# Linear attention: a pair's state updates one piece ahead of its outputs, and row tiles loaded one half per piece

## The chip, the core and the metric

The kernel runs on one NeuronCore of a Trainium2 chip. TensorE (PE in the profile; PEld is its weight load) multiplies matrices into PSUM; VectorE (DVE), ScalarE (ACT) and GpSimd (POOL) work on tiles element by element; SyncE (SP) issues most of the DMA transfers, ScalarE's queue some of them. Each engine takes its own instructions in order, and semaphores hold an instruction until its operands are there and its output buffer is free. The metric is the device time of one execution in microseconds (us), the median of several.

## The reference, cut to what matters

One decoder layer: a normalised input goes through one large projection, then through two branches side by side (a state space model, SSD, and a gated linear attention, GLA), which are gated, merged, projected and added to the input. The change lies in the linear attention and in how the normalised input is made. Per head, with the sequence cut into chunks:

```python
def step(s, inp):
    qi, ki, vi, gi = inp                       # gi: cumulated log gates of the chunk
    o_inter = einsum('bhtk,bhkv->bhtv', qi * exp(gi), s)
    att = ...                                  # causal, decayed q k products in the chunk
    o_intra = einsum('bhts,bhsv->bhtv', att, vi)
    g_last = gi[:, :, -1]
    k_dec = ki * exp(g_last[:, :, None, :] - gi)
    s_new = exp(g_last)[..., None] * s + einsum('bhsk,bhsv->bhkv', k_dec, vi)
    return s_new, o_inter + o_intra
```

So a chunk's output needs the state `s` from before the chunk, and the state goes on by a decay and an increment that depends on keys and values alone. The input of the branches is `u = x * rsqrt(mean(x*x) + eps) * w`, row by row. Sequence 2048 plus 16 meta tokens, model width 1024, 4 GLA heads with 128 key and 256 value channels, 16 SSD heads in 4 groups.

## The kernel before, in words

The sequence is cut into four blocks of 512 rows (the first has the 16 meta rows as well), and a block into four chunks of 128. The program has two halves.

The **first half** goes over the blocks. For each block it goes over eight units: four SSD groups (`ssd_proj`) and four GLA heads (`gla_proj`). A unit is mostly projections: TensorE multiplies weight tiles (`whl`, loaded by SyncE in `load_w`) with the normalised block `u`, in three matmuls per product (`accum`, L185 to L187: high by high, high by low, low by high). A unit is written as a generator that yields six times, that is, in six *pieces*. After every piece the loop calls `step()`, which advances each generator in `running` by one of its own pieces: the scan of the unit before (`ssd_scan` or `gla_scan`), the load of the next block (`fetch_u`, which runs `load_u`, begun with the first GLA head), and sums for the second half. A scan of a head h is begun when its projections are over, so its piece 1 stands behind the first projection piece of head h+1, its piece 7 behind the first projection piece of head h+2, beside piece 1 of the next scan. The last scan of all is begun earlier, within its own head.

TensorE and SyncE keep exactly this written order (`manual_schedule`). The order of ScalarE, VectorE and GpSimd is set by a planner that simulates the program with its own costs.

`gla_scan` of one head: pieces 1 to 5 build the attention matrix in six levels (`level_in`: L688 to L695 on VectorE, L691 and L692 on ScalarE; `level_out`: two matmuls L703 into a `pc` bank, merged by L710), and turn the decayed keys around (`turn_keys`, L724, giving `kdt`). Piece 6 transposes the odd chunks of the attention matrix (L790) and splits them into `atp`. Pieces 7 and 8 take a pair of chunks each:

- six matmuls `kdt` by values into a `pc` bank, the increments of the two chunks;
- for the first chunk the state update L805 on VectorE (old state times decay plus increment) into a tile `c1` (the profile calls it `c`), the output's matmul with the old state (L808), three matmuls with the first chunk's attention, three with the second's;
- last the matmul with the new state (L811). The second update writes `s_gla`, the state's own tile.

Then ScalarE copies the outputs (L812) and squares them (L815). PSUM has two `pc` banks; they are used by `level_out`, by the increments, by the outputs and by the SSD scan (L564 and L567).

`load_u` of a block behind the first: in each of four pieces it loads one row chunk in two halves of 512 columns (L258, tile `acc`, two buffers, which the convolution of the SSD groups uses too), squares each half with a row sum on ScalarE (L259), adds the sums (L260) and raises the mean to the power -1/2 (on GpSimd). Then one piece turns the row factors into a broadcast tile (L280), and eight pieces load one feature tile each (L294), scale it (L296), write its high part (L298) and its low part (L300) and store it (L299).

`dt_chain`, once per block, computes step sizes and their cumulated sums with four small scratch tiles of the pool `sm` and writes the block's tiles `tkd`, `tkc`, `wde`, `ecu`, `dec`.

The **second half** (from L876) is a series of large products from operands in DRAM. Its tiles take the memory of the first half's. Between the halves the last two scans end beside a few first products (`between`).

Of the kernel before, what the change touches and what calls it, by code (L numbers as in the profile page):

```python
# [7 lines left out]
F32 = mybir.dt.float32  # L8
# [3 lines left out]
AF = mybir.ActivationFunctionType  # L12
ALU = mybir.AluOpType

P = 128
D = 1024
KT = 8
META = 16
BLK = 512
NCH = BLK // P  # L20
# [5 lines left out]
NSQ = 5  # L26
NT4 = 5
NACT = 8
NC1 = 6
LEVELS = (64, 32, 16, 8, 4, 2)  # L30
NMSK = len(LEVELS) + 1
QSCALE = 128.0 ** -0.5
# [8 lines left out]
def trunk_kernel(ctx: ExitStack, tc: tile.TileContext, xm, xmt, w_feat, w_tok, w_zm, w_br, w_o,  # L41
                 cf32, cmsk, pvec, fnw, hvec, gw2, out):
    nc = tc.nc
# [5 lines left out]
    def mk(pool, shape, dt, tag, **kw):  # L49
        cnt[0] += 1  # L50
        return pool.tile(shape, dt, tag=tag, name=f"{tag}_{cnt[0]}", **kw)
# [52 lines left out]
    for s in range(nsb):  # L104
        b = 2 * s + 2
# [16 lines left out]
    bpool, wk, sm, const = pool1("bpool", 1), pool1("wk", 2), pool1("sm", 4), pool1("const", 1)  # L122
    pj = ctx.enter_context(tc.tile_pool(name="pj", bufs=3, space=bass.MemoryType.PSUM))
    pt = ctx.enter_context(tc.tile_pool(name="pt", bufs=3, space=bass.MemoryType.PSUM))
    pc = ctx.enter_context(tc.tile_pool(name="pc", bufs=2, space=bass.MemoryType.PSUM))

    def bank(pool, tag):
        return mk(pool, [P, 512], F32, tag)
# [20 lines left out]
    s_gla = const.tile([P, GH, 256], F32, name="s_gla")  # L149
# [33 lines left out]
    def accum(ps, stat, mov, first, last, **kw):  # L183
        (sh, sl), (mh, ml) = stat, mov
        nc.tensor.matmul(ps, sh, mh, start=first, stop=False, **kw)  # L185
        nc.tensor.matmul(ps, sh, ml, start=False, stop=False, **kw)  # L186
        nc.tensor.matmul(ps, sl, mh, start=False, stop=last, **kw)  # L187
# [44 lines left out]
    def split(h, lo, src):  # L232
        nc.scalar.activation(h, src, AF.Copy)
        nc.vector.tensor_tensor(lo, src, h.bitcast(F32), op=ALU.subtract)


    def load_u(b):
        m0 = META if b == 0 else 0
        row0 = META - m0 + b * BLK
        tt = m0 + BLK  # L240
        pair = mk(upool, [P, 2, KT * (META + BLK)], F32R, "u")[:, :, :KT * tt]
        uh, ul = [pair[:, i].rearrange("p (k t) -> p k t", k=KT) for i in range(2)]

        def rows_rstd(r0, n, vector=False):
            ss = mk(sm, [P, 1], F32, "ss")
            if m0:
                xt = mk(wk, [P, D], F32, "tok4", bufs=NT4)
                nc.sync.dma_start(xt[:n], xm[r0:r0 + n, :])
                if vector:
                    nc.vector.scalar_tensor_tensor(xt[:n], xt[:n], 1.0, xt[:n], op0=ALU.mult, op1=ALU.mult,  # L250
                                                   accum_out=ss[:n])
                else:
                    nc.scalar.activation(xt[:n], xt[:n], AF.Square, accum_out=ss[:n])
            else:
                s2 = mk(sm, [P, 2], F32, "ss2")
                for i in range(2):
                    xt = mk(wk, [P, META + BLK], F32, "acc")[:, :BLK]
                    nc.sync.dma_start(xt, xm[r0:r0 + n, i * BLK:(i + 1) * BLK])  # L258
                    nc.scalar.activation(xt, xt, AF.Square, accum_out=s2[:, i:i + 1])  # L259
                nc.vector.tensor_tensor(ss, s2[:, 0:1], s2[:, 1:2], op=ALU.add)  # L260
            r = mk(sm, [P, 1], F32, "rs1")
            nc.vector.tensor_scalar(r[:n], ss[:n], 1.0 / D, EPS, op0=ALU.mult, op1=ALU.add)
            nc.gpsimd.tensor_tensor(r[:n], r[:n], mhalf[:n, 0:1], op=ALU.pow)
            return r

        rs = []
        if m0:
            rm_s = rows_rstd(0, META, True)
        for c in range(NCH):
            rs.append(rows_rstd(META + b * BLK + c * P, P, c % 2))  # L270
            yield
        if m0:
            rs.append(rm_s)
            nc.sync.dma_start(cst[:, :2], cf32[:, :2])
            nc.sync.dma_start(pv, pvec)
            for q in range(NWR):
                raws[f"zm_{q}"] = load_raw(w_zm[:, q * 288:(q + 1) * 288])
        rb = bank(pt, "pt")
        for c in range(NCH):
            nc.tensor.matmul(rb[:, c * P:(c + 1) * P], rs[c].to_broadcast([P, P]), ident, start=True, stop=True)  # L280
        rbs = [(rb, m0, BLK)]
        if m0:
            rm = bank(pt, "pt")
            nc.tensor.matmul(rm[:, :META], rs[NCH][:META].to_broadcast([META, P]), ident[:META, :META],
                             start=True, stop=True)
            rbs = [(rm, 0, META)] + rbs
        else:
            rbc = mk(wk, [P, 3 + META + BLK], F32, "cin")[:, :BLK]
            nc.scalar.activation(rbc, rb, AF.Copy)
            rbs = [(rbc, 0, BLK)]  # L290
            yield
        for kt in range(KT):
            xk = mk(wk, [P, META + BLK], F32, "act" if m0 else "acc", bufs=NACT if m0 else 2)[:, :tt]
            nc.sync.dma_start(xk, xmt[:, kt, row0:row0 + tt])  # L294
            for ps, a, n in rbs:
                nc.vector.scalar_tensor_tensor(xk[:, a:a + n], xk[:, a:a + n], norm_w[:, kt:kt + 1], ps[:, :n],  # L296
                                               op0=ALU.mult, op1=ALU.mult)
            nc.scalar.activation(uh[:, kt, :tt], xk, AF.Copy)  # L298
            nc.scalar.dma_start(u_left[b][kt], xk[:, m0:])  # L299
            nc.vector.tensor_tensor(ul[:, kt, :tt], xk, uh[:, kt, :tt].bitcast(F32), op=ALU.subtract)  # L300
            yield
        return uh, ul
# [62 lines left out]
    def dt_chain(o, psd):  # L365
        m0, nck, ci0 = o.m0, o.nck, o.ci0
        tkd, tkc, wde, ecu, dec = o.tkd, o.tkc, o.wde, o.ecu, o.dec

        def t80(tag):
            return mk(sm, [P, 5, NH], F32, tag, bufs=1)[:, :nck]  # L370

        x = t80("dx")
        for i in range(nck):
            nc.vector.tensor_tensor(x[:, i], psd[i][:, 256:272], hv[:, 0], op=ALU.add)
            nc.scalar.activation(
                o.alr[:, i].rearrange("p (r c) -> p r c", c=16),
                psd[i][:, 272:288].unsqueeze(1).to_broadcast([P, 3, 16]), AF.Copy)
        e = t80("de")
        nc.scalar.activation(e, x, AF.Abs)
        nc.scalar.activation(e, e, AF.Exp, scale=-1.0)  # L380
        w1 = t80("dw")
        nc.vector.tensor_scalar(w1, e, 1.0, None, op0=ALU.add)
        ln = t80("dl")
        nc.scalar.activation(ln, w1, AF.Ln)
        nc.vector.scalar_tensor_tensor(e, w1, 1.0, e, op0=ALU.subtract, op1=ALU.subtract)
        nc.vector.tensor_tensor(ln, ln, e, op=ALU.subtract)
# [8 lines left out]
        if m0:  # L395
            nc.tensor.matmul(ps[:, :NH], ones[:META], x[:META, 0], start=True, stop=True)
        nc.tensor.matmul(ps[:, ci0 * NH:nck * NH], ones, x[:, ci0:].rearrange("p c h -> p (c h)"),
                         start=True, stop=True)
# [245 lines left out]
    def gla_scan(o, h, qs, kf, vt, vm, gs, last=False):  # L644
        m0, tt = o.m0, o.tt
# [16 lines left out]
        egl = mk(sm, [P, NCH], F32, "egl")  # L662
        nc.scalar.activation(egl, gl[:, :NCH], AF.Exp)
        qg = mk(wk, [P, META + BLK], F32, "act", bufs=NACT)[:, :BLK]
# [6 lines left out]

        xa = mk(wk, [P, 2, P], F32, "c1", bufs=NC1)
        kqs = {}
# [45 lines left out]
        kdt = []  # L719
# [63 lines left out]
        atp = [mk(wk, [P, NCH, P], F32R, "atp", bufs=2) for _ in range(2)]  # L783
# [5 lines left out]
        for r in range(2):  # L789
            nc.tensor.transpose(ps[:, r * P:(r + 1) * P], att[:, 2 * r + 1], ident)  # L790
        split(*[t[:, 1::2] for t in atp], ps[:, :256].rearrange("p (c t) -> p c t", t=P))
        yield

        ot = mk(wk, [P, NCH, 256], F32, "ot", bufs=1)
        ssq = mk(sm, [P, 4], F32, "ssq")
        s_old = s_gla[:, h]
        for c0 in range(0, NCH, 2):
            two = range(c0, c0 + 2)
            inc, po = [bank(pc, "pc").rearrange("p (c f) -> p c f", c=2) for _ in range(2)]
            vc = [[t[:, c] for t in vt] for c in two]  # L800
            for i, c in enumerate(two):
                accum(inc[:, i], [t[:, c] for t in kdt], vc[i], True, True)
            states = [s_old, mk(wk, [P, 256], F32, "c1", bufs=NC1), s_old]
            for i, c in enumerate(two):
                nc.vector.scalar_tensor_tensor(states[i + 1], states[i], egl[:, c:c + 1], inc[:, i],  # L805
                                               op0=ALU.mult, op1=ALU.add)
                if i == 0:
                    nc.tensor.matmul(po[:, 0], qg[:, c * P:(c + 1) * P], s_old, start=True, stop=False)  # L808
                    accum(po[:, 0], [t[:, c] for t in atp], vc[0], False, True)
                    accum(po[:, 1], [t[:, c + 1] for t in atp], vc[1], True, False)  # L810
                    nc.tensor.matmul(po[:, 1], qg[:, (c + 1) * P:(c + 2) * P], states[1], start=False, stop=True)  # L811
            nc.scalar.activation(ot[:, c0:c0 + 2], po, AF.Copy)  # L812
            for i, c in enumerate(two):
                jk = mk(wk, [P, 256], BF16, "junk", bufs=1)
                nc.scalar.activation(jk, po[:, i], AF.Square, accum_out=ssq[:, c:c + 1])  # L815
            yield
# [265 lines left out]
    for si, st in enumerate(stages):  # L1082
        for q in range(0 if si else 8, 28):
            p, j = PS[q // 4], q % 4
# [9 lines left out]
    for key, st in zip(late, (stages[0], stages[-4])):  # L1094
        i, end = begins[stages.index(st)] + 9, begins[stages.index(st) + 1] - 16
# [145 lines left out]
```

## Time and profile before

| | us |
|---|---|
| median of 3 runs (lowest to highest) | 2324.8 (2320.24 to 2333.66) |
| the profiled execution | 2331.51 |
| its span, first to last instruction | 2329.4 |
| TensorE busy | 2244.1 |
| VectorE busy | 1555.6 |
| ScalarE busy | 1182.2 |
| GpSimd busy | 680.8 |
| mean granted TensorE clock | 0.988 |

All engine times are of the one profiled execution, which was 6.7 us above the median. The first half ends at about 1543 us. A row of the timeline gives start, duration, engine, line, operation, what it writes and reads, shape, and in square brackets how long the engine stood idle before it and what ended that. A row of the waits gives engine, tile and line, what was waited for, total us, number, longest. "clock" is the TensorE clock that the chip granted, 1.00 being full speed.

### The profile page before, as it was taken

To read this page: it belongs to the slowest core of one execution; us is meant where nothing else is said; L and a number is where in the kernel's file an instruction comes from. 1 tells how busy PE (TensorE), PEld (TensorE's weight loads), DVE (VectorE), ACT (ScalarE), POOL (GpSimd) and SP (SyncE) were. 2 spreads that over 40 slices of the span, in tenths; PEclk is the share of its full clock that TensorE was granted. 3 is DMA by queue.
4 is the path that set the end of the run, shared out by engine and by line. 5 is a ranking of instruction groups with operands and counts; after the bars stand their busy time and mean duration, and the time that the engine had idled before them with its cause. 6 is when DMAs were issued, how large, how long until landed. Compare 5 with 4: busy or idle time off the path is not lost. (4 is left out here: it accounts for less than half of the span.)

```text
span 2329.4 us, 36518 instructions
## 1 busy us (share of the span) xinstructions
PE 2244.1 (96%) x12641; PEld 1955.6 (84%) x12641; DVE 1555.6 (67%) x2895; ACT 1182.2 (51%) x2726; POOL 680.8 (29%) x681
## 2 busy tenths in 40 slices
PE   7899999999999999999999999889999999999897
PEld 6899889888889989888988898768888888888776
DVE  5676766676675676566567555664578945788766
ACT  4666654465543455543465443554554545554443
POOL 4344433122222122211122100037324264323331
PEclk9999999999999999999999999989999999999999
DMA  8666866767786676776676645457577866677743
GB/s 305 227 204 213 294 225 206 224 193 243 246 274 187 216 219 214 260 259 209 195 231 216 206 166 164 137 194 231 186 258 266 306 225 220 235 279 253 244 147 119
DMA packets 301544, 518.04 MB, mean 222 GB/s; under 512 B 27696, under 2 KB 143664, under 8 KB 301360
## 3 DMA queue, kind: packets, MB, share of 16 engines
q1 hardware_dynamic: 200400, 402.84, 53.1%
q10 hardware_dynamic: 100960, 112.88, 14.0%
q8 instruction: 99, 1.62, 0.3%
q14 instruction: 85, 0.70, 0.1%
HBM read 368.42 MB, written 147.19 MB: 221 GB/s over the span
## 5 line engine op out<-in xcount | busy, mean ns | idle before, releaser
L185 PE MATMUL pj<-u,whl 128*128 128x512 f32 (+1 forms) x1184 | 449.0, 379 | 16.1 <-ACT acc L475 6.6
L187 PE MATMUL pj<-u,whl 128*128 128x512 f32 (+1 forms) x1184 | 432.9, 366 | 1.7 <-POOL whl L166 0.8
L186 PE MATMUL pj<-u,whl 128*128 128x512 f32 (+1 forms) x1184 | 431.8, 365 | 0.0
L185 PE MATMUL pj<-whl,u 128*128 128x256 f32 (+1 forms) x992 | 289.6, 292 | 2.3 <-ACT u L298 1.5
L187 PE MATMUL pj<-whl,u 128*128 128x256 f32 (+1 forms) x992 | 282.8, 285 | 1.5 <-DVE u L300 1.5
L186 PE MATMUL pj<-whl,u 128*128 128x256 f32 (+1 forms) x992 | 282.6, 285 | 0.9 <-POOL whl L166 0.9
L185 PEld LDWEIGHTS pj<-u,whl 128*128 128x128 f32 x1184 | 226.3, 191 | 55.4 <-ACT acc L475 7.7
L185 PE MATMUL pj<-b,a 128*128 128x512 f32 x640 | 254.3, 398 | 15.4 <-ACT sn L953 8.9
L187 PEld LDWEIGHTS pj<-u,whl 128*128 128x128 f32 x1184 | 225.8, 191 | 38.1 <-POOL whl L166 2.1
L186 PEld LDWEIGHTS pj<-u,whl 128*128 128x128 f32 x1184 | 226.6, 191 | 33.8
L187 PE MATMUL pj<-b,a 128*128 128x512 f32 x640 | 252.9, 395 | 0.0
L186 PE MATMUL pj<-b,a 128*128 128x512 f32 x640 | 251.9, 394 | 0.0
L185 PEld LDWEIGHTS pj<-whl,u 128*128 128x128 f32 x992 | 190.2, 192 | 3.7 <-ACT u L298 1.8
L80 POOL TENSOR_TENSOR wr<-wr 128x256 f32<-128x256 f32 x80 | 67.4, 843 | 428.3 <-DMA wr<-y 176.0
L187 PEld LDWEIGHTS pj<-whl,u 128*128 128x128 f32 x992 | 190.1, 192 | 2.2 <-DVE u L300 2.2
L186 PEld LDWEIGHTS pj<-whl,u 128*128 128x128 f32 x992 | 190.4, 192 | 1.6 <-POOL whl L166 1.1
L166 POOL TENSOR_TENSOR whl<-wr,whl 128x512 fp32r<-128x512 f32 (+1 forms) x100 | 134.5, 1352 | 186.5 <-ACT whl L165 139.0
L912 DVE TENSOR_TENSOR b<-br,b 128x512 fp32r<-128x512 f32 x196 | 153.6, 803 | 48.8 <-ACT b L911 48.2
L927 POOL TENSOR_TENSOR as<-ar,ar 128x512 f32<-128x512 f32 x40 | 57.4, 1436 | 414.7 <-DMA ar<-in_w_br 162.6
L479 DVE SCALAR_TENSOR_TENSOR acc<-cin,hcw,acc 128x512 f32<-128x512 f32 (+1 forms) x192 | 154.3, 804 | 32.0 <-ACT acc L475 31.1
L911 ACT ACTIVATE b<-br 128x512 fp32r<-128x512 f32 x196 | 119.6, 626 | 103.8 <-DMA br<-br_t 37.1
L937 DVE TENSOR_TENSOR a<-ar,a 128x512 fp32r<-128x512 f32 x160 | 128.0, 807 | 61.6 <-ACT a L936 60.8
(277 smaller groups left out, 5061.2 us busy)
## 6 DMA issues: line engine op xcount, KB each, us to landing
whl<-k_s SPq DMA_DIRECT2D x96, 512.0 KB, 4.3
whl<-k_g SPq DMA_DIRECT2D x96, 512.0 KB, 4.2
whl<-k_v SPq DMA_DIRECT2D x48, 512.0 KB, 3.8
whl<-k_z SPq DMA_DIRECT2D x36, 512.0 KB, 3.8
wr<-in_w_feat SPq DMA_DIRECT2D x64, 256.0 KB, 4.5
k_s<-whl SPq DMA_DIRECT2D x32, 512.0 KB, 3.6
cb<-cumd ACTq DMA_DIRECT2D x64, 256.0 KB, 5.6
y<-gg ACTq DMA_DIRECT2D x64, 256.0 KB, 4.7
```

What stands on the lines that cost most here:

```text
L80: nc.gpsimd.tensor_tensor(o, x, y, op=ALU.subtract)
L166: nc.gpsimd.tensor_tensor(hl[:, 1], raw, hl[:, 0].bitcast(F32), op=ALU.subtract)
L185: nc.tensor.matmul(ps, sh, mh, start=first, stop=False, **kw)
L186: nc.tensor.matmul(ps, sh, ml, start=False, stop=False, **kw)
L187: nc.tensor.matmul(ps, sl, mh, start=False, stop=last, **kw)
L479: nc.vector.scalar_tensor_tensor(acc, cin[:, k:k + tt], hcw[:, ti, k:k + 1], acc, op0=ALU.mult, op1=ALU.add)
L911: nc.scalar.activation(t[:, 0], raw, AF.Copy)
L912: nc.vector.tensor_tensor(t[:, 1], raw, t[:, 0].bitcast(F32), op=ALU.subtract)
L927: nc.gpsimd.tensor_tensor(s1, a21, a22, op=ALU.add)
L937: nc.vector.tensor_tensor(t[:, 1], src, t[:, 0].bitcast(F32), op=ALU.subtract)
```

## The change

Three edits.

1. In `gla_scan` a helper `advance(c0)` issues the increments of a pair and its two state updates, each new state in a tile `c1` of its own (the last one in `s_gla`). `advance(0)` stands at the end of piece 6, behind the transposes; `advance(2)` stands in piece 7, behind the output matmuls of the first pair. In an output the matmul with the state comes first for both chunks, the three with the attention after it. `c1` gets 8 buffers instead of 6.
2. In `load_u` of the blocks 1 to 3 each row chunk's two halves are loaded and squared in two pieces, so that this part takes eight pieces and the rest comes four pieces later.
3. `dt_chain` uses the block's `ecu`, `wde`, `tkc` and `dec` for its four scratch values instead of tiles of their own.

```diff
-NC1 = 6
+NC1 = 8
...
+        def rows_load(r0, n, i=None):
+            xt = mk(wk, [P, D], F32, "tok4", bufs=NT4) if i is None else mk(wk, [P, META + BLK], F32, "acc")[:, :BLK]
+            nc.sync.dma_start(xt[:n], xm[r0:r0 + n, :] if i is None else xm[r0:r0 + n, i * BLK:(i + 1) * BLK])
+            return xt
+
+        def rstd_rows(ss, n):
             r = mk(sm, [P, 1], F32, "rs1")
             nc.vector.tensor_scalar(r[:n], ss[:n], 1.0 / D, EPS, op0=ALU.mult, op1=ALU.add)
             nc.gpsimd.tensor_tensor(r[:n], r[:n], mhalf[:n, 0:1], op=ALU.pow)
             return r
...
-        for c in range(NCH):
-            rs.append(rows_rstd(META + b * BLK + c * P, P, c % 2))
-            yield
+            for c in range(NCH):
+                rs.append(rows_rstd(META + b * BLK + c * P, P, c % 2))
+        else:
+            for c in range(NCH):
+                s2 = mk(sm, [P, 2], F32, "ss2")
+                for i in range(2):
+                    xt = rows_load(META + b * BLK + c * P, P, i)
+                    nc.scalar.activation(xt, xt, AF.Square, accum_out=s2[:, i:i + 1])
+                    if i == 0:
+                        yield
+                ss = mk(sm, [P, 1], F32, "ss")
+                nc.vector.tensor_tensor(ss, s2[:, 0:1], s2[:, 1:2], op=ALU.add)
+                rs.append(rstd_rows(ss, P))
+                yield
...
-        x = t80("dx")
+        x = ecu[:, :nck]
...
-        e = t80("de")
+        e = wde[:, :nck]
...
-        w1 = t80("dw")
+        w1 = tkc[:, :nck]
...
-        ln = t80("dl")
+        ln = dec[:, :nck]
...
         split(*[t[:, 1::2] for t in atp], ps[:, :256].rearrange("p (c t) -> p c t", t=P))
-        yield
-
+        def advance(c0):
+            inc = bank(pc, "pc").rearrange("p (c f) -> p c f", c=2)
+            for i in range(2):
+                accum(inc[:, i], [t[:, c0 + i] for t in kdt], [t[:, c0 + i] for t in vt], True, True)
+            for i in range(2):
+                c = c0 + i
+                states.append(mk(wk, [P, 256], F32, "c1", bufs=NC1) if c < NCH - 1 else s_gla[:, h])
+                nc.vector.scalar_tensor_tensor(states[c + 1], states[c], egl[:, c:c + 1], inc[:, i],
+                                               op0=ALU.mult, op1=ALU.add)
+
+        states = [s_gla[:, h]]
+        advance(0)
+        yield
         ot = mk(wk, [P, NCH, 256], F32, "ot", bufs=1)
         ssq = mk(sm, [P, 4], F32, "ssq")
-        s_old = s_gla[:, h]
         for c0 in range(0, NCH, 2):
             two = range(c0, c0 + 2)
-            inc, po = [bank(pc, "pc").rearrange("p (c f) -> p c f", c=2) for _ in range(2)]
-            vc = [[t[:, c] for t in vt] for c in two]
+            po = bank(pc, "pc").rearrange("p (c f) -> p c f", c=2)
             for i, c in enumerate(two):
-                accum(inc[:, i], [t[:, c] for t in kdt], vc[i], True, True)
-            states = [s_old, mk(wk, [P, 256], F32, "c1", bufs=NC1), s_old]
-            for i, c in enumerate(two):
-                nc.vector.scalar_tensor_tensor(states[i + 1], states[i], egl[:, c:c + 1], inc[:, i],
-                                               op0=ALU.mult, op1=ALU.add)
-                if i == 0:
-                    nc.tensor.matmul(po[:, 0], qg[:, c * P:(c + 1) * P], s_old, start=True, stop=False)
-                    accum(po[:, 0], [t[:, c] for t in atp], vc[0], False, True)
-                    accum(po[:, 1], [t[:, c + 1] for t in atp], vc[1], True, False)
-                    nc.tensor.matmul(po[:, 1], qg[:, (c + 1) * P:(c + 2) * P], states[1], start=False, stop=True)
+                nc.tensor.matmul(po[:, i], qg[:, c * P:(c + 1) * P], states[c], start=True, stop=False)
+                accum(po[:, i], [t[:, c] for t in atp], [t[:, c] for t in vt], False, True)
+            if c0 == 0:
+                advance(2)
             nc.scalar.activation(ot[:, c0:c0 + 2], po, AF.Copy)
```

More of the change, by code (lines that the diff above doesn't have):

```diff
@@ L242, in load_u @@
         uh, ul = [pair[:, i].rearrange("p (k t) -> p k t", k=KT) for i in range(2)]
[L244 to L260, printed above, removed]
+        def rows_load(r0, n, i=None):
[3 more added lines that the diff above has]
+        def rstd_rows(ss, n):
             r = mk(sm, [P, 1], F32, "rs1")
@@ L264, in rows_rstd @@
             return r
+        def rows_rstd(r0, n, vector):
+            ss = mk(sm, [P, 1], F32, "ss")
+            xt = rows_load(r0, n)
+            if vector:
+                nc.vector.scalar_tensor_tensor(xt[:n], xt[:n], 1.0, xt[:n], op0=ALU.mult, op1=ALU.mult,
+                                               accum_out=ss[:n])
+            else:
+                nc.scalar.activation(xt[:n], xt[:n], AF.Square, accum_out=ss[:n])
+            return rstd_rows(ss, n)
         rs = []
@@ L268, in load_u @@
             rm_s = rows_rstd(0, META, True)
-        for c in range(NCH):
-            rs.append(rows_rstd(META + b * BLK + c * P, P, c % 2))
-            yield
+            for c in range(NCH):
+                rs.append(rows_rstd(META + b * BLK + c * P, P, c % 2))
+        else:
+            for c in range(NCH):
[5 more added lines that the diff above has]
+                        yield
+                ss = mk(sm, [P, 1], F32, "ss")
+                nc.vector.tensor_tensor(ss, s2[:, 0:1], s2[:, 1:2], op=ALU.add)
+                rs.append(rstd_rows(ss, P))
+                yield
         if m0:
```

## The prediction

> **What bounds the kernel now.** I read the page first, then TensorE's waits, then the places of those waits in the timeline, then SyncE's waits. The page:
>
> ```profile
> PE 2244.1 (96%) x12641; PEld 1955.6 (84%) x12641; DVE 1555.6 (67%) x2895; ACT 1182.2 (51%) x2726; POOL 680.8 (29%) x681
> ```
>
> TensorE (PE) is busy 96% of the span. The change adds and removes no matmul, so all it can move is the remaining 4%: time in which PE stands still, and time in which it runs at a lower granted clock. Of PE's waits (line, what it waited for: us in total, times, longest) these lie on lines that the change touches or feeds:
>
> ```profile
> PE pc L811 <- DVE c L805: 8.8, 5, 2.8
> PE pj L185 <- DMA whl<-k_g: 2.6, 2, 1.5
> PE pc L564 <- DVE sq L555: 2.7, 2, 1.7
> PE pj L187 <- DVE dw L382: 0.8, 1, 0.8
> PE pt L724 <- DVE act L661: 1.6, 2, 1.0
> PE pc L808 <- DVE c L710: 1.3, 1, 1.3
> PE pc L703 <- ACT junk L815: 4.3, 1, 4.3
> ```
>
> The first is the state of the linear attention. The timeline of PE, and then of VectorE (DVE), at its first occurrence:
>
> ```profile
> 322.48 0.28 PE L185 MATMUL pc<-tok,kdt 128*128 128x256 f32 x1
> ...
> 323.07 0.28 PE L187 MATMUL pc<-tok,kdt 128*128 128x256 f32 x1
> 323.19 0.59 PE L808 MATMUL pc<-s_gla,act 128*128 128x256 f32 x2
> ...
> 324.20 0.28 PE L187 MATMUL pc<-tok,atp 128*128 128x256 f32 x1
> 327.27 0.70 PE L811 MATMUL pc<-c,act 128*128 128x256 f32 x2 [2.79 <-DVE c L805]
> ```
>
> ```profile
> 326.13 0.69 DVE L688 TENSOR_TENSOR sq<-g_all 128x512 f32<-128x512 f32 x1
> 326.74 0.47 DVE L805 SCALAR_TENSOR_TENSOR c<-s_gla,egl,pc 128x256 f32<-128x256 f32 x1
> ```
>
> The six increment matmuls (`pc<-tok,kdt`) are over by 323.2. The product with the new state (L811) is ready for PE by 324.3, but DVE has other work (L688 of the next head's scan) in front of the state update and starts it only at 326.74. Thus PE's in-order queue, and all the projection behind it, waits 2.79 us. The same place one and two blocks later:
>
> ```profile
> 696.65 0.70 PE L811 MATMUL pc<-c,act 128*128 128x256 f32 x2 [2.44 <-DVE c L805]
> 1060.26 1.22 PE L811 MATMUL pc<-c,act 128*128 128x256 f32 x2 [2.67 <-DVE c L805]
> ```
>
> All three are head 0's scan, whose first output piece falls at the start of head 2. The busy time per head's stretch (start:end, length, then busy us and instructions of PE, PEld, DVE, ACT, POOL, then granted clock, DMA share, GB/s) shows what is different there: the first three rows are heads 1, 2 and 3 of block 1, the last two are heads 1 and 2 of block 3, in which no next block is loaded.
>
> ```profile
> 652.60:697.00 44.40, 40.98 (x253) 36.39 (x251) 31.76 (x65) 19.79 (x48) 7.89 (x9) 1.00 0.88 290
> 697.00:741.30 44.30, 44.30 (x267) 39.62 (x266) 27.11 (x58) 15.51 (x42) 7.60 (x9) 0.96 0.62 193
> 741.30:785.00 43.70, 43.70 (x292) 40.39 (x292) 26.10 (x60) 17.88 (x49) 7.64 (x9) 1.00 0.56 174
> 1371.00:1414.60 43.60, 43.60 (x265) 38.90 (x264) 22.30 (x57) 18.06 (x46) 1.01 (x1) 1.00 0.52 172
> 1414.60:1457.40 42.80, 42.80 (x268) 38.53 (x267) 23.21 (x58) 16.78 (x45) 1.59 (x1) 1.00 0.53 161
> ```
>
> Without the load PE never stands; with it, head 1 loses 44.40 - 40.98 = 3.4 us, which is 2.44 at L811 and 1.0 at L724. The clock falls after some of these waits (same columns):
>
> ```profile
> 697.90:701.20 3.30, 3.30 (x9) 2.62 (x8) 0.48 (x1) 1.12 (x5) 0.00 (x0) 0.50 0.00 0
> 1060.30:1066.50 6.20, 6.20 (x15) 4.86 (x16) 1.68 (x3) 2.46 (x8) 0.00 (x0) 0.50 0.00 0
> 984.80:988.00 3.20, 3.20 (x14) 2.96 (x13) 1.33 (x3) 1.62 (x4) 3.04 (x4) 0.51 0.93 251
> 327.30:330.70 3.40, 3.40 (x26) 3.35 (x27) 1.70 (x3) 3.06 (x10) 1.67 (x1) 1.00 0.09 27
> ```
>
> After two of the three long waits PE ran at half clock for 3.3 and 6.2 us; after the one at 327 it did not.
>
> The second thing is SyncE (SP), which issues the loads in written order. Its timeline at the start of head 0 in blocks 1 and 2, its waits there in block 1, and PE's price:
>
> ```profile
> 598.54 4.20 SPq L258 DMA_DIRECT2D acc<-in_xm  x2
> 602.84 0.85 SPq L161 DMA_DIRECT2D whl<-k_g  x2
> ...
> 957.61 6.05 SPq L258 DMA_DIRECT2D acc<-in_xm  x2
> 963.78 0.82 SPq L161 DMA_DIRECT2D whl<-k_g  x2
> ```
>
> ```profile
> SPq L258 <- ACT acc L259: 8.6, 4, 3.5
> SPq L258 <- DVE act L483: 4.5, 1, 4.5
> ```
>
> ```profile
> 606.91 0.50 PE L185 MATMUL pj<-u,whl 128*128 128x512 f32 x1 [1.47 <-DMA whl<-k_g]
> 967.68 0.50 PE L185 MATMUL pj<-u,whl 128*128 128x512 f32 x1 [1.14 <-DMA whl<-k_g]
> ```
>
> The first row half waits 4.5 us for a buffer of the convolution, the second 3.5 us for the first half's Square (L259), and the weight loads stand behind both. PE reaches the weights before they land.
>
> **The change part by part.**
>
> *State one piece ahead.* Per scan the same 12 increment matmuls, 4 products with the state, 12 with the attention matrix and 4 updates of 0.47 us are issued, only placed otherwise: PE's and DVE's work is unchanged, 0. The first pair's six increments now come behind the transposes of the piece before; their updates have a projection piece to finish in (a sixth of a head, 44.3/6 = 7.4 us, against 324.3 - 323.2 = 1.1 us of cover before). DVE was late by at most 2.79, so the wait of L811 goes: **-8.8 us**. The increment of the second pair stands behind the first pair's outputs, with nothing on PE waiting for it until the next piece. If the updates were later than 7.4 us, L808 of the next piece would wait; nothing of the trace is that late. PSUM: the bank of an increment is freed by the updates before the next scan's L703 wants it. So this part adds no wait in the steady state.
>
> With two of those waits go their half-clock stretches, (3.3 + 6.2)/2 = **-4.75 us**, because at a granted clock of 0.5 half of the time is lost. The Trainium skill, in "TensorE: Matmul & The Clock Gate", section HAM oscillation, gives the rule that it is PE-idle gaps above about 3.4 us that throttle. By that rule waits of 2.4 to 2.8 us would cost no clock, and the sum would be about 5 us smaller. This trace disagrees: the rows show clock 0.50 right behind waits of 2.44 and 2.67 us. That the wait at 327 left the clock at 1.00 fits the same page's statement that the monitor's window runs free.
>
> *Buffers.* `c1` goes from 6 to 8 and a scan takes 7 of them, not 6; no instruction. Four scratch tiles of the step-size chain become the block's own tiles: same instructions, once per block, and the last write (`ecu`) already stood behind the matmul that reads `x`. Between -0.8 (the wait on `dw` above) and +4 x 0.8 us; I take 0. The sizes also shift where the second half's tiles lie over the first half's, which no row shows: a load that comes to lie over a tile freed later starts later, and I count that in the tail's bounds.
>
> *Row tiles, one half per piece.* The same 24 loads, Squares and sums, in eight pieces of a block and not four. Behind the first half SP goes on to the weights after the 4.5 us wait, 3.5 us (block 1) and some 5 us (block 2, whose two issues took 6.05) sooner than now, more than PE's 1.47 and 1.14: **-2.6 us**. Later pieces have one row load in front of the weights instead of two. ScalarE has one Square less in each piece:
>
> ```profile
> L259 ACT ACTIVATE acc<-acc x24: 610/628/637, 218.7 to 987.6; 128x512 f32<-128x512 f32 x24
> L259 ACT ACTIVATION_READ_ACCUMULATOR acc<-acc x24: 184/186/200, 219.2 to 988.2; 128x1 f32 x24
> 621.88 1.10 PE L564 MATMUL pc<-c,sq 128*128 128x64 f32 x8 [1.04 <-DVE sq L555]
> ```
>
> L564 waits for a decay matrix that ScalarE makes behind those Squares. One Square with its read is 0.81 us; over two blocks 1.6 us, and half of the 1.6 us that the half clock at 984.80 costs: **-2.4 us** (bounds 0 and -4.3).
>
> The rest of the load comes four pieces later: the eight feature tiles, each of one L296 and one L300 on DVE, a copy and a store on ScalarE and a load on SP, which lay beside heads 0 and 1, now reach to the fifth piece of head 2.
>
> ```profile
> L296 DVE SCALAR_TENSOR_TENSOR acc<-acc,pv,cin x24: 735/751/1744, 264.9 to 1053.2; 128x512 f32<-128x512 f32 x24
> L300 DVE TENSOR_TENSOR u<-acc,u x24: 676/689/695, 266.6 to 1056.1; 128x512 fp32r<-128x512 f32 x24
> ```
>
> Five tiles of 0.75 + 0.69 us put 7.2 us more DVE work into head 2: 27.1 + 7.2 = 34 of 44.3 us, above the 31.8 of today's head 1, which cost PE 1.0 us without L811. I take 1.3 us in each of three blocks, +4.0, and the L724 waits of today (1.6) go from head 1: net **+2.4 us**, bounds -1.6 and +3 x 3.4 = +10 (if head 2 then loses what head 1 loses now). The normalised block, and its copy in DRAM that the next block's sums read, are still complete a head (44 us) before their use. Each row's power on GpSimd has a piece until L280 needs the last; without that cover PE would wait there for one DVE and one GpSimd instruction.
>
> *Tail.* At the end of the first half the last two scans run with little beside them. L808 and L703 wait there for PSUM banks (1.3, 4.3). The same banks are taken in another order, and the last scan's increments stand behind its keys' split. I take 0, bounds -4 (they go) and +4 (another such wait).
>
> **Sum:** -8.8 - 4.75 - 2.6 - 2.4 + 2.4 = -16.15, say -16 us. The profiled execution took 2331.5 us (span 2329.4), 6.7 above the median 2324.8 of the three runs shown; there -16 gives 2315, and on the median **2309**.
>
> **Rivals.** (a) *The half clock stays.* If the stretches at 0.50 don't follow from these waits, only the waits go: -16 + 4.75 + 0.8 = -10.6, 2314. For it: one of three long waits left the clock alone. Against: the other two have it at once. The clock-gate page of the Trainium skill, by its 3.4 us, is on this side.
> (b) *DVE's lateness moves on.* DVE had no gap before 326.74; the work ahead of the update stays, and PE, 2.8 us earlier, may meet it at the next bank. Half of 13.55 comes back: -9.4, 2315. Against it: behind the waits DVE has little left; in the rows at 697.90 and 1060.30 it is busy 0.48 of 3.30 and 1.68 of 6.20 us.
> (c) *The change doesn't do what it says.* The planner sets DVE's order; if it puts the updates a whole piece later, L811 and L808 wait as now: -16 + 13.55 = -2.6, 2322. Against it: they can be placed only by their operands, which come a piece sooner.
> (d) *Slower:* the feature tiles overload DVE in head 2. Five pieces in three blocks, each losing the mean of today's long waits (2.63 us): +39 against -16, 2348. It decides from 16/15 = 1.1 us per piece, and is measurable from 1.8. For it: 34 us of DVE work is more than any head has now. Against: 34 of 44.3 leaves ten, and today's 31.8 cost 1.0.
>
> **How the numbers follow.** Forecast 0.52, (a) 0.14, (b) 0.14, (c) 0.11, (d) 0.09. About 0.5% (11.6 us) can be told from no change. The forecast alone is faster by more; its own range is 2297 to 2313. (a), (b) and (c) lie within 0.5%, together 0.39; (d) is slower. The range for 8 in 10 goes from 2296 (L564 and the tail gain too) to 2327: it takes in (a), (b), (c) with the tail's +4, and leaves out (d) and what little lies below.
>
> **What the changed profile would show.** No PE wait at the last product of `qg` in a piece, above all near 327, 696, 1060; granted clock 1.00 there. SP's two row loads apart, no PE wait on `whl<-k_g` near 607 and 967. L564's waits below 1 us. L296 reaching into head 2 with PE busy there above 43 of 44.3 us. I am wrong if PE's waits appear at L724, L773 or L790 in head 2, if the second half's tail is longer, or if the clock is at 0.50 as often as now.

## The result, and the profile after

The changed kernel takes 2304.4 us (median of 5 runs, 2300.1 to 2307.8), the kernel before 2324.8 (5 runs). The ratio is 0.9906, with a 95% interval from 0.9877 to 0.9934: about 20 us, 0.9%, faster. The prediction said 2309 with a range from 2296 to 2327.

The profiled execution took 2306.7 us, its span is 2304.9, against 2329.4 before. So the two profiled executions lie further apart than the medians do, 24.8 against 20.4 us. The page's first part, engine lines:

```profile
PE 2236.0 (97%) x12641; PEld 1954.7 (85%) x12641; DVE 1546.8 (67%) x2895; ACT 1181.4 (51%) x2726; POOL 677.5 (29%) x681
```

The instruction counts are the same, engine by engine. What changed is where TensorE (PE) stands still. In the following I call *middle stretch* the part from the second SSD group of block 0 to the last weight matmul of the first half; it holds every scan but the last two's ends. PE in the middle stretch and in the tail of the last scans (start:end, length, PE busy us and instructions, clock, DMA share, GB/s), first of before, then of after:

```profile
210.80:1493.00 1282.20, 1262.25 (x7802) 0.99 0.67 218
1493.00:1542.60 49.60, 32.08 (x162) 0.88 0.40 129
```

```profile
211.90:1471.20 1259.30, 1252.80 (x7802) 1.00 0.69 222
1471.20:1519.50 48.30, 31.77 (x162) 0.88 0.40 132
```

Of the 24.5 us between the two spans 22.9 lie in the middle stretch. PE's idle time there falls from 20.0 to 6.5 us (length less busy). Its busy time falls by 9.5 us with equal counts. Before, three parts of the stretch ran at clock 0.50 (their rows stand in the prediction: 3.3, 6.2 and 3.2 us, together 12.7), now none. Half of 12.7 is 6.4, so 3.1 of the 9.5 us are not explained by the clock. PE's waits in the middle stretch, all that the view lists, after:

```profile
PE pc L185 <- DVE c L809: 2.5, 3, 1.4
PE pt L402 <- DVE ecu L399: 2.1, 2, 1.1
PE pc L713 <- DVE s_gla L747: 0.6, 1, 0.6
PE pt L290 <- ACT gg L611: 0.4, 1, 0.4
PE pj L185 <- DMA whl<-k_zm: 0.3, 1, 0.3
```

Lines have moved by some ten: L809 is the state update (L805 before), L821 the product with a state, L402 the cumulated sums of the step sizes, L713 `level_out`, L800 the transposes of the odd chunks, L246 the row loads, L574 the SSD product. The waits of L811, L564, L724, L790 and on `whl<-k_g` are gone. The first entry is new, and it stands exactly where L811 waited. PE and then VectorE (DVE) at the start of head 2 in block 0:

```profile
314.52 0.28 PE L187 MATMUL pc<-tok,kdt 128*128 128x256 f32 x1
...
321.00 0.59 PE L821 MATMUL pc<-c,act 128*128 128x256 f32 x2
...
321.66 0.28 PE L187 MATMUL pc<-tok,atp 128*128 128x256 f32 x1
323.32 0.38 PE L185 MATMUL pc<-tok,kdt 128*128 128x256 f32 x1 [1.38 <-DVE c L809]
```

```profile
319.38 0.47 DVE L809 SCALAR_TENSOR_TENSOR c<-s_gla,egl,pc 128x256 f32<-128x256 f32 x1
322.80 0.47 DVE L809 SCALAR_TENSOR_TENSOR c<-c,egl,pc 128x256 f32<-128x256 f32 x1
```

The first pair's increments end at 314.8, DVE makes the first update at 319.38 and the second at 322.80, 8 us after the increment that it adds. The outputs (L821) no longer mind: the one that takes the first new state starts at 321.00. But the second pair's increments want the PSUM bank that the second update still has to read, and PE waits 1.38 us. At 686 and 1040 it is 0.59 and 0.50 us. The granted clock stays up after all three:

```profile
320.20:327.00 6.80, 5.42 (x41) 1.00 0.87 304
684.10:690.90 6.80, 6.21 (x34) 1.00 0.65 223
1038.20:1045.00 6.80, 6.30 (x34) 1.00 0.72 230
```

SyncE (SP) at the start of head 0 of block 1, after: one row half, then the weights, then a piece later the next half.

```profile
592.58 0.33 SPq L246 DMA_DIRECT2D acc<-in_xm  x1
593.02 1.01 SPq L161 DMA_DIRECT2D whl<-k_g  x2
597.26 0.33 SPq L246 DMA_DIRECT2D acc<-in_xm  x1
```

### The profile page after: what moved, and what is told of

Read it like the earlier page. It is cut to its first block, busy times and chain, and to the rows that moved or that the text cites. A ratio compares the mean times of both kernels' runs of the same rounds, so it can differ in the third digit from the quotient of the medians.

```text
span 2304.9 us, 36458 instructions
## 1 busy us (share of the span) xinstructions
PE 2236.0 (97%) x12641; PEld 1954.7 (85%) x12641; DVE 1546.8 (67%) x2895; ACT 1181.4 (51%) x2726; POOL 677.5 (29%) x681
## 4 chain that ended last, share of the span: by engine, by line
PE 78%; DMA 7%; DVE 6%; ACT 4%; issue 3%; POOL 1%; SPq 0%; ACTq 0%; DVEq 0%; POOLq 0%
PE pj L185 18%; PE pj L187 18%; PE pj L186 18%; PE pt L185 3%; PE pt L187 3%; PE pt L186 3%; PE pc L574 2%; PE pc L185 2%; PE pc L186 2%; PE pc L187 2%; PE pc L713 2%; DMA br<-out_t 1%; PE pc L575 1%; PE pc L577 1%; DMA acc<-in_xmt 1%
## 5 line engine op out<-in xcount | busy, mean ns | idle before, releaser
L925 DVE TENSOR_TENSOR b<-br,b 128x512 fp32r<-128x512 f32 x196 | 154.8, 810 | 50.3 <-ACT b L924 49.6
```

The lines of the kernel that those rows point to most:

```text
L925: nc.vector.tensor_tensor(t[:, 1], raw, t[:, 0].bitcast(F32), op=ALU.subtract)
```

## The experiments

Each kernel was timed in five rounds beside the kernel before; ratios are to that kernel, with 95% intervals.

### The parts alone

Theory: the states and the row tiles each take away their own waits. Rivals: one part does nearly all; the two need each other; the new buffers do it.

**States one piece ahead alone** (row tiles as before, both halves in a piece):

```diff
+            for c in range(NCH):
+                rs.append(rows_rstd(META + b * BLK + c * P, P, c % 2))
+                yield
```

> Only the states one piece ahead (with the 8 buffers and the block's tiles as scratch); row tiles loaded as before, both halves in a piece. If the two parts act by themselves: the waits of L811 (8.8 us) and the 4.75 us of half clock go, less about 2.5 us of new waits of the second pair's increments for their PSUM bank, so some -11 us, ratio 0.995; the waits on the weights at 607 and 968 and of the SSD output on its decay matrix stay. If the row tiles bring nearly all of it: -3 us or less, 0.999. If the new order needs the later feature tiles to pay: slower than that, with new waits in head 2.

Measured: 0.998 (0.9965 to 0.9995), 2318.2 against 2323.9. This was surprisingly little, so it was run once more, on another chip.

> The states one piece ahead alone, once more. Alone they gave 0.998, although taking away the wait of L811 alone gave 0.995, and with the row tiles the order is the other way round (0.991 against 0.993). If the first of these was low by chance: 0.995 to 0.996, and the two parts nearly add up. If alone it really brings less: 0.997 to 0.999 again.

Measured: 0.9976 (0.9961 to 0.9991). It really brings only 5 to 6 us alone. PE's longest waits in the middle stretch of the first of these runs:

```profile
PE pc L564 <- DVE sq L555: 3.6, 2, 2.5
PE pj L185 <- DMA whl<-k_g: 2.7, 2, 1.8
PE pt L392 <- DVE ecu L389: 2.1, 2, 1.0
PE pc L703 <- DVE s_gla L737: 1.8, 2, 1.2
PE pc L185 <- DVE c L799: 1.8, 2, 0.9
```

L811's 8.8 us are gone, but 5.7 us in three new entries came for it (the cumulated sums, the bank of the meta state, the bank of the increments; together 4.1 in the second run), and L564, which was 2.7, is 3.6 (3.2 in the second). The entry of the meta state is not the states' own: the kernel with the buffers alone has it as well, with 1.3 us.

**Row tiles one half per piece alone** (states and outputs in one piece as before):

```diff
-        states = [s_gla[:, h]]
-        advance(0)
-        yield
+        yield
```

> Only the row tiles one half per piece (with the 8 buffers and the block's tiles as scratch); states and outputs in one piece as before. If the two parts act by themselves: the weights in time (2.6), the SSD output (2.7 and 1.7 of half clock), the waits of the keys' transposes (1.6) and some of the GpSimd-split weights of block 0 (1.7) go, some -10 us, ratio 0.996, and L811 still waits 6 us or more with its half clock, since a feature tile still falls on the start of head 2. If it is the load of the next block alone that makes VectorE late there, and its shift cures it: L811's waits go too, -18 us or more, 0.992. If the later feature tiles overload head 2: new waits there, 1.000 or above.

Measured: 0.9971 (0.9956 to 0.9986). PE's waits in the middle stretch, all that the view lists, the clock right behind the three long ones, and DVE ahead of the second of them:

```profile
PE pc L821 <- DVE c L815: 11.2, 6, 3.6
PE pt L290 <- ACT gg L611: 0.4, 1, 0.4
PE pc L713 <- DVE s_gla L747: 0.2, 1, 0.2
```

```profile
321.20:324.10 2.90, 2.90 (x11) 0.50 0.59 201
689.50:692.60 3.10, 3.10 (x7) 0.50 0.10 35
1047.70:1051.00 3.30, 3.30 (x8) 0.50 0.11 41
```

```profile
686.32 0.74 DVE L306 SCALAR_TENSOR_TENSOR acc<-acc,pv,cin 128x512 f32<-128x512 f32 x1
...
687.76 0.69 DVE L310 TENSOR_TENSOR u<-acc,u 128x512 fp32r<-128x512 f32 x1
...
688.97 0.47 DVE L815 SCALAR_TENSOR_TENSOR c<-s_gla,egl,pc 128x256 f32<-128x256 f32 x1
```

Everything that the row tiles were to take away is away. The product with the new state (here L821) waits longer than before, 11.2 against 8.8 us (9.0 with the buffers alone). The rows show a reason: PE's increments are over by 684.8, and between them and the update (L815) DVE now works on a feature tile that came later (L306 and L310, 1.4 us together). It is the same at 1044 to 1046, and one L306 stands there at 319.60; in the kernel before, no feature tile's instruction starts between increments and update at the three places. So the row tiles do not cure that wait, and their later feature tiles lengthen it.

**Buffers and scratch alone:**

```diff
-NC1 = 6
+NC1 = 8
...
-        x = t80("dx")
+        x = ecu[:, :nck]
```

> Only the 8 buffers of c1 and the block's tiles as scratch; states and row tiles as before. If these edits only make room: within 3 us of before, ratio 0.999 to 1.001, the same waits. If the two more buffers help the SSD scan, which uses three per chunk, or the moved addresses help the second half: -5 us or more.

Measured: 1.001 (0.9997 to 1.0022). These edits only make room.

**The whole change with the old scratch tiles and 7 buffers:**

```diff
-NC1 = 8
+NC1 = 7
...
-        x = ecu[:, :nck]
+        x = t80("dx")
```

> The whole change, but the step-size chain keeps its own four scratch tiles and c1 has 7 buffers, one for each that a scan takes. If the waits of the cumulated sums' matmul on the chain (2.1 us after, none before) come from the shared tiles: they go, 2 us faster than the whole change, ratio 0.989 to 0.990. If they come from VectorE's order, which the later feature tiles changed: they stay and the ratio is that of the whole change, 0.991.

Measured: 0.9912 (0.9895 to 0.993), as the change. The new wait of the cumulated sums is still there, now on the old tile:

```profile
PE pt L402 <- DVE dx L399: 2.1, 2, 1.0
```

So it does not come from sharing tiles. It comes with the states, since the buffers alone and the row tiles alone don't have it. What in VectorE's planned order puts it there was not separated.

### What the price of L811 is

**The kernel before, with the old state in L811:**

```diff
-                    nc.tensor.matmul(po[:, 1], qg[:, (c + 1) * P:(c + 2) * P], states[1], start=False, stop=True)
+                    nc.tensor.matmul(po[:, 1], qg[:, (c + 1) * P:(c + 2) * P], s_old, start=False, stop=True)
```

> The kernel before, in which the second chunk of a pair is multiplied with the old state instead of the new one (so half of the chunks are given the state of one chunk earlier): nothing on PE waits for a state update of its own piece, and nothing else is moved. If the waits of L811 cost what they measure: all 8.8 us and the half clock go, -9 to -13 us, ratio 0.995. If VectorE's and SyncE's lateness only moves on to the next instruction that needs them: about half of that, as the states alone gave (-5 us, 0.998), with longer waits on weights, on the decay matrix or on PSUM.

This kernel gives half of the chunks a state that lacks one chunk's update, so its output is not the layer's; only its time is of use. Measured: 0.9951 (0.9937 to 0.9966), 2315.1 against 2324.9, some 10 us. The middle stretch of this run has no time at clock 0.50. L811's 8.8 us are gone, and 3.0 us in entries that this stretch did not have before came for them:

```profile
PE pc L524 <- DVE s_gla L805: 1.7, 3, 0.6
PE pc L703 <- DVE s_gla L805: 0.8, 3, 0.3
PE pc L703 <- DVE s_gla L737: 0.5, 1, 0.5
```

With the 4.75 us of half clock that makes 8.8 - 3.0 + 4.75 = 10.6 us, near what was measured. So the wait costs about what it measures, with its half clock. The gain is nearly twice that of the states alone; what makes the difference is taken up under what stays open.

**The same with the row tiles one half per piece** (on the kernel with the row tiles alone):

```diff
-                    nc.tensor.matmul(po[:, 1], qg[:, (c + 1) * P:(c + 2) * P], states[1], start=False, stop=True)
+                    nc.tensor.matmul(po[:, 1], qg[:, (c + 1) * P:(c + 2) * P], s_old, start=False, stop=True)
```

> The row tiles one half per piece, states and outputs in one piece as before, and the second chunk of a pair multiplied with the old state (the state of one chunk earlier), so that L811 waits for nothing. If the two parts gave together more than each alone because the waits that one leaves grow when the other is gone: the whole gain of the change or a little more, ratio 0.988 to 0.991, though the parts alone gave 0.995 (old state) and 0.997 (row tiles), which would make 0.992. If they only add: 0.992 to 0.993.

This kernel, too, leaves out one chunk's update for half of the chunks. Measured: 0.993 (0.9912 to 0.9947). That is what the two ratios alone make, 0.9951 x 0.9971 = 0.992: they only add. My reason for a larger sum, that each wait grows when the other goes, is seen in the single waits (8.8 to 11.2, 2.7 to 3.6) but does not show in this sum.

### Spacing or shift of the row tiles

**Both halves in a piece again, then four empty pieces:**

```diff
-                    if i == 0:
-                        yield
...
+            for _ in range(4):
+                yield
```

> The whole change, but both halves of a row tile are loaded in one piece again, followed by four empty pieces, so that the feature tiles come where the change has them. If the spacing of the halves is what the row tiles bring (weights in time, one Square less ahead of the decay matrix): the waits at 607 and 968 on the weights (2 to 3 us) and of the SSD output (2 to 4 us with half clock) come back, 5 to 8 us slower than the change, ratio 0.994. If the later feature tiles are what brings it: as the change, 0.991, and the waits of the keys' transposes stay away.

Measured: 0.9966 (0.9952 to 0.998), 2317.4, some 14 us slower than the change and so more than I expected of the spacing. SP at the start of head 0 of block 1, and PE's longest waits in the middle stretch:

```profile
594.37 5.02 SPq L246 DMA_DIRECT2D acc<-in_xm  x2
599.49 0.85 SPq L161 DMA_DIRECT2D whl<-k_g  x2
```

```profile
PE pc L574 <- DVE sq L565: 4.3, 2, 2.9
PE pj L185 <- DMA whl<-k_g: 2.5, 2, 1.9
```

With the halves together the weights stand behind the second half again and the SSD product (L574) waits for its decay matrix again. The later feature tiles do one thing alone: the waits of the transposed keys (L724 before) stay away here too. Of the 14 us the middle stretch shows 7.6 (1266.9 against 1259.3), the tail 2.0; the profiled executions (2315.3 and 2304.9 in span) don't hold the rest.

### Two further steps

**The first pair's increments a piece earlier still** (end of piece 5, but for the last scan):

```diff
         split(*[t[:, 0::2] for t in atp], att[:, 0::2])
...
+        states = [s_gla[:, h]]
+        if not last:
+            advance(0)
         yield
         if last:
             turn_keys()
...
-        advance(0)
+        if last:
+            advance(0)
         yield
```

> The whole change, with the first pair's increments and updates a further piece earlier (end of piece 5; the last scan as in the change). If the second pair's increments wait for their bank (2.5 us in the three blocks) because VectorE comes to the first pair's updates late, and a further piece is cover enough: those waits go, 2 to 3 us faster than the change, ratio 0.989. If the planner puts the updates as late as before, whatever their operands: the waits stay, 0.991. If updates taken earlier only push VectorE's other work back: other waits (keys' transposes, cumulated sums) of the same size, 0.991 or above.

Measured: 0.9887 (0.9869 to 0.9905), 2299.6. The waits of the increments for their bank are gone from the middle stretch; what is left there:

```profile
PE pt L402 <- DVE ecu L399: 2.1, 2, 1.0
PE pc L713 <- DVE s_gla L747: 0.6, 1, 0.6
PE pt L290 <- ACT gg L611: 0.4, 1, 0.4
```

**The load of the next block begun one piece later:**

```diff
-            if i == SG and b + 1 < nblk:
-                begin(fetch_u(b + 1))
...
                 step()
+                if (i, n) == (SG, 0) and b + 1 < nblk:
+                    begin(fetch_u(b + 1))
```

> The whole change, with the load of the next block begun one piece later, so that the first row half no longer holds SyncE until the convolution's buffer is free. If SyncE's standing still (3.5 to 13.9 us per block) costs PE nothing any more since the weights behind it land in time: as the change, 0.991. If it still delays weights that ScalarE and GpSimd must split in block 0: 1 to 2 us faster, 0.990. If the feature tiles, now to the end of head 2, meet more of VectorE's work there: slower, 0.993.

Measured: 0.9895 (0.988 to 0.9909), 2301.2. The bank waits nearly go here too (0.14 us is left, at 322). The feature tiles then fall on other pieces of VectorE's work; that this is why was not tested.

**Both, and the change once more on the same chip:**

> The first pair's increments a further piece earlier, and the load of the next block begun one piece later, both on top of the change. What either removed in the steady part (2.8 us of 6.5 us of PE waits) were the same waits of the second pair's increments for their bank, so together they give no more than either: 4 to 5 us faster than the change, ratio 0.988. If they add: 0.987 or less.

Measured: 0.9887 (0.9867 to 0.9906), 2298.8 against 2324.8.

> The change as it is, beside the two others on the same chip: 0.991 again, 4 us slower than with both further steps.

Measured: 0.9907 (0.989 to 0.9924), 2302.2. Both steps together are 3.4 us below the change on the same chip, and no better than the earlier increments alone. The intervals overlap, so that either step beats the change is likely and not shown.

## Why the prediction was right

- **State, -8.8:** the wait of L811 went, as forecast, but the sentences "nothing of the trace is that late" and "So this part adds no wait in the steady state" failed. The second update comes 8 us behind its increment, more than the 7.4 us of a piece, and 2.5 us came back as the bank wait. The cover was also smaller than I had it, since pieces differ in length: from the end of the increments it is 5.4 us to the outputs (314.80 to 320.21) and 7.1 to where the second pair wants the bank (321.94). At 686 the second update came only 7.1 us behind its increment (678.81 to 685.90), within my 7.4, and PE waited all the same. The next reader I had named for such a case was the product with the state; it was the PSUM bank of the second pair. A further 2.1 came at L402. So the term measured -4.2. A part of rival (b), lateness that moves on, is true.
- **Half clock, -4.75:** right for the change as a whole. All 12.7 us at 0.50 left the middle stretch, the part at 984 (1.6 us, counted with L564 below) among them, so that behind L811 the 4.75 are right and in all it is 6.4; rival (a) falls. Taking L811's wait away alone also left none, and with the row tiles alone each of the three long waits (2.70, 3.57 and 3.35 us) has its 3 us at 0.50. The mean clock of all runs agrees for the change (4 to 6 us less are lost to it) and not for the states by themselves (see what stays open). The Trainium skill, "TensorE: Matmul & The Clock Gate", section HAM oscillation, has idle gaps above about 3.4 us throttle. The measurement goes against that figure: two of these three are shorter, and so were those of 2.44 and 2.67 us before.
- **Weights in time, -2.6:** right, all of it went, and in block 0 two waits on weights split by GpSimd (0.9 and 0.8) with it, which I had not counted. With the halves together 2.5 came back.
- **L564, -2.4:** the mechanism was right and the size too small: all 2.7 us went, and the 1.6 of half clock behind, together 4.3, which was my bound.
- **Later feature tiles, +2.4:** this term failed. Head 2 of block 1 now has DVE busy 32 us (I had said 34) and PE loses next to nothing:

```profile
643.00:686.40 43.40, 42.84 (x265) 38.25 (x263) 27.82 (x62) 18.38 (x45) 8.37 (x10) 1.00 0.85 276
686.40:730.00 43.60, 43.57 (x271) 39.28 (x272) 32.05 (x69) 19.29 (x52) 8.27 (x9) 1.00 0.77 249
```

The first row is head 1, the second head 2. As I read it, it is not the busy sum of a stretch that decides, but whether something has to be ready within its own piece: with the row tiles alone, where the update still has to be, the later tiles do cost PE, 11.2 against 8.8 us at the product with the state. The L724 waits went as I had said, so the term is -1.6. Some of the bank wait counted under the state may be theirs (an L310 of 0.68 us stands between the two updates at 319.77); that was not separated. Rival (d) falls.

- **Buffers, 0**, and **tail, 0:** right (1.001; 49.6 to 48.3 us).
- **Rival (c):** falls in the main, though in the sentence "it puts the updates a whole piece later" it describes the second update rightly.

Of the sum, the terms that were too large (state) and too small (L564, feature tiles, the weights of block 0) nearly cancel, which made -16 of some -20. That the sum came nearer than its terms is luck.

**What stays open.** The two parts alone give 0.998 (0.9976 the second time) and 0.9971, which make 0.995; together they give 0.9906, 0.9907 and, with the old scratch tiles, 0.9912. That is 8 to 10 us more than the parts; the intervals barely meet. The one traced execution of each run does not settle it. The middle stretch is 1282.2 us before, 1272.9 and 1268.3 in the two runs with the states, 1271.0 with the row tiles and 1259.3 with both. So the states are worth -9.3 or -13.9 there and the row tiles -11.2, against -22.9 for both. Against the kernel with the buffers alone (1278.1) it is -5.2 or -9.8, and -7.1, against -18.8.

The span and the mean granted clock are on record for every run, not only for the traced ones. Span times (1 - clock) is an estimate of the time lost to the lower clock, since at 0.50 half of the time is lost (after, at 1520.5, matmuls of 512 columns follow each other by 0.43 us at that clock, at 318 by 0.23 at full clock); the clock is given to 0.001, which is 2.3 us of a span. Means over the runs:

| | lost to the clock, us | rest of the span, us |
|---|---|---|
| before, on three chips | 27.8 to 29.1 | 2293.8 to 2294.2 |
| states alone, two runs | 28.4, 28.4 | 2288.2, 2288.9 |
| row tiles alone | 29.3 | 2285.8 |
| the change, two runs | 23.9, 22.2 | 2278.5, 2279.2 |
| the change with the old scratch tiles | 24.2 | 2276.3 |
| old state in L811 | 23.9 | 2288.3 |
| row tiles and old state | 25.4 | 2281.1 |

In the rest the parts about add up: 5 to 6 us and 8 us alone, 15 to 18 together. Most of the surplus is clock: neither part alone lowers its loss, and together they save 4 to 6 us. The same column separates the states alone from the old state in L811, whose rests are alike. Where in the program the states alone still lose that time, and why, was not shown.

## What to carry to other kernels

A wait inside one piece of a written order has next to no cover (1.1 us here), whatever the mean load of the engine it waits for; moving the producer a piece ahead gives it cover, but look also at who wants the producer's *buffer* next. In a queue that issues loads in order, put one load that has to wait for a buffer in a piece, and the urgent loads behind it; two such loads in a row make everything behind them wait for the first one's whole round trip. And test parts alone before adding up, with the granted clock beside the time: here each part alone left the time lost to the clock as it was, and both together took about a sixth of it.

## What the runs showed of the hardware

In the middle stretches of all 14 traces (before, after and the twelve runs) TensorE has 12 waits of 2.0 to 3.6 us. Eight of them were followed, within 1.3 us of their end, by 3.4 us at a granted clock of 0.50 (one, of 2.67 us, by 6.8); those of 2.07, 2.15, 2.79 and 2.88 us were not. Of the waits between 1.0 and 2.0 us only two were, of 1.30 and 1.66 us. A short wait can so cost its length again, or more: half of the 6.8 us behind the wait of 2.67 us is 3.4. By the mean clock of all runs the kernel before loses some 28 us to the lower clock, the changed kernel 22 to 24.
